# The key's rotation on all 128 partitions, in three steps, and the queries' rotation two gates earlier

## The chip, the cores and the metric

The kernel runs on one core of a Trainium2 chip. The metric is the device time of one execution in microseconds. The core has a matrix engine (TensorE, PE in the profile), three engines for elementwise work (VectorE or DVE, ScalarE or ACT, GpSimd or POOL), and a queue engine (SyncE, SP) that here only issues DMA transfers. Each engine works through its own list of instructions in a fixed order. PSUM holds what TensorE produces, in banks; a tile of 128x1024 takes two of them.

## What is computed

A two-layer encoder on one sequence of 1024 tokens with 1024 features. Each layer normalizes, projects into many pieces, runs two kinds of heads side by side, and projects back:

```
for i in range(DEPTH):                       # 2 layers
    u = rmsnorm(h, ln_mix[i]) @ w_in[i]
    c_q, c_kv, k_rope, gate_a, gq, gk, gv, lr_f, lr_b, gate_g = split_cols(u)
    y_mla = mla_branch(c_q, c_kv, k_rope, pos, ...) * silu(gate_a)
    y_gla = gla_branch(gq, gk, gv, lr_f, lr_b, ...) * silu(gate_g)
    h = h + concat(y_mla, y_gla) @ w_out[i]
    h = h + sigmoid(rmsnorm(h, ple_norm[i]) @ w_ple_gate[i]) * (p[i] @ w_ple_proj[i])

def apply_rope(x, pos):                      # 32 + 32 features, one angle per feature and token
    x1, x2 = x[..., :32], x[..., 32:]
    return concat([x1 * cos - x2 * sin, x1 * sin + x2 * cos])

# mla_branch: scores of 4 heads = q_nope . k_nope + q_rope . k_r, then softmax, then @ v
# q_rope = apply_rope(of each head's 64 features); k_r = apply_rope(k_rope), one for all heads
# gla_branch: linear attention with decay, forward and backward, in chunks of 64
```

The rotary key `k_rope` is one of the first things projected in a layer; its rotation is needed only by the scores.

## The kernel before

Activations lie with features on the partitions and tokens along the free dimension, so most tiles are 128x1024 f32. Each float operand of a product is split into a high and a low part (`wh`, `wl` for weights, `kh`, `kll` for keys, `qh`, `ql` for queries, `rh`, `rl` for the rotated queries, `ks`, `kl` for the rotated key), and a product is three matmuls: high by high, low by high, high by low. Splitting is a cast on ScalarE (L129, L132) and a subtraction on VectorE (L130, L133). Weights are loaded by SP into `wr` (L145) and split on ScalarE (L146, L150) and by GpSimd's accumulating DMA (L151); they rotate through two raw buffers and five split ones. Nearly all other tiles come from one ring of 41 buffers.

Within a layer the work is cut in steps. Two strings in `ORDER`, one for each layer, name them in the order in which they are handed to a scheduler, which then fixes each engine's list. A capital letter with a digit is a step: Q and K project queries and keys of the linear heads, V values, Z the decays of head i, S its states, O its output, G and A gate tiles, C and D latent tiles, N and M their norms. X (`q_pairs`) projects the rotary parts of all four heads into two PSUM tiles `xx` and loads the cosine and sine tables; E (`rotary_key`) rotates the key; T (`rotary_queries`) rotates the queries; H (`q_head`) and k (`make_k`) make one head's queries and keys; s, b, v and y are scores, turned probabilities, values and outputs of attention. A plus sign behind a step puts its PSUM tile into the other of two pools, `mm` and `aux`, of two tiles each. `xx` lives in `aux` until T has read it.

The steps around the change:

- `rotary_tables` (R) computes sine and cosine once, in a work tile whose 128 partitions hold 4 quarters of the tokens by 32 features (128x256), and writes them to device memory, `sind` and `cosd` (L278).
- X loads both tables back, four copies of 32x1024 each (L580).
- E works on rows 64 to 128 of `small`, the tile that holds the key's two halves of 32 features: four products, a difference and a sum on 32 partitions (L588 to L593), then two casts (L595, L596) and two subtractions (L598) that put the result twice into the 128 partitions of `ks` and `kl`.
- T reads `xx` (L613, L614, L615, twice), splits, and copies the parts to the tiles `qs` of four heads with sixteen copies on SP (L623).
- Scores `s0` (L672) of head 0 multiply, for each of 4 blocks of tokens and 2 halves of keys, `qh` and `ql` by `kh`, `qh` by `kll`, and `qs` by `ks` and by `kl`: 40 matmuls.
- Z (`gla_decay`): on ScalarE z, a, exp, log (L382 to L385), on VectorE z, two scans and more (L386 to L410). Its result goes through S and O to a norm that needs `sqh` (L132), `sql` (L133) and a product on TensorE (L185).

Of the kernel before, what the change touches and what calls it, by code (L numbers as in the profile page):

```python
# [46 lines left out]


WTAG = "aux"
ORDER = ("K0 R0 Q0 G0+ Z0 V0 K1 S0 Z1 V1 O0 S1 Q1 D0 Z2 G1 G2 P0 O1 S2 C0 Z3 D1 C1 N0 D2 O2 S3 G3 M0 A0 O3 X0 A1 E0 A2 A3+ H0 k0 T0 s0 v0 H2 k1+ s1 k2 b0 H1 k3 s2 y1 b1 H3+ s3 b2 v1 s4 y0 y3 b3 y2 s5 b4 w0 w1+ s6 w2 b5 w3+ s7 w4 b6 w5+ s8 w6 w7 b7",  # L50
         "Q0 K0 Z0 V0 S0 Z1 V1 S1 Q1 K1 Z2 G0 O0 S2 G1 Z3 G2+ C0 O1 D0 O2 S3 G3 C1 N0 D1 D2+ O3 M0 X0 A0 A1 E0 A2 k0 y2 H0 A3 T0 s0 v0 H3 k1+ s1 H1 b0 H2 s2 k2 b1 s3 y0 k3+ b2 v1 s4 y3 y1 b3 s5 b4 w0 w1+ s6 w2+ b5 w3 s7 w4 b6 w5+ s8 w6+ w7 b7")

ENG = dict(at="V", qi="V", qb="P", og="P", gate="P", sq="V", kT="A", put="A", o="A", ple="A", hadd="V")
TCKW = {"schedule_with_timeline_sim": True}
# [3 lines left out]
def hybrid_encoder(ctx: ExitStack, tc: tile.TileContext, xT, pT, pos, vecs, w_in, wq, wk, wv,  # L58
                   wz, w_out, w_gate, w_proj, outT, dbg=None):
    nc = tc.nc  # L60
    dbg = dbg or {}

    cp = ctx.enter_context(tc.tile_pool(name="const", bufs=1))
# [5 lines left out]
    def dram(shape, name):  # L69
        return tc.dram_tile(shape, F32, name=name)  # L70
# [49 lines left out]
    def mt(dt=F32, name="mt"):  # L120
        return rp.tile([P, S], dt, tag="r", name=name)
# [100 lines left out]
    h1d = dram([8, P, S], "h1d")  # L222
    cosd = dram([32, S], "cosd")
    sind = dram([32, S], "sind")

    def ple_projection(i):
        ops = []
# [12 lines left out]
        for g in range(4):  # L240
            hi, lo = load_split(w_proj[i, g], HC)
            for c in range(2):
# [4 lines left out]
                copy("ple", o, flat(ps))  # L247
                nc.sync.dma_start(projd[i][g * 2 + c], o)

    def rotary_tables():  # L250

        n = S // 4

        work = mt(name="rot")
        kk, ang, *rs = (work[:, i * n:(i + 1) * n] for i in range(4))
        posi = kk.bitcast(I32)
        for b in range(4):
            nc.sync.dma_start(posi[b * 32:(b + 1) * 32], pos[:, b * n:(b + 1) * n].to_broadcast((32, n)))
        nc.vector.tensor_copy(ang, posi)
        nc.vector.tensor_scalar(ang, ang, vec[:, V_INV:V_INV + 1], None, op0=ALU.mult)  # L260
        MAGIC = 12582912.0
        TWO_PI = 2.0 * np.pi
        C1 = 6.28125
        C2 = float(np.float32(np.round((TWO_PI - C1) * 2 ** 20) / 2 ** 20))
        C3 = float(np.float32(TWO_PI - C1 - C2))
        for r, dst, quarter in zip(rs, (sind, cosd), (0.0, 0.25)):
            nc.vector.tensor_scalar(kk, ang, 1.0 / TWO_PI, quarter, op0=ALU.mult, op1=ALU.add)
            nc.vector.tensor_scalar(kk, kk, MAGIC, None, op0=ALU.add)
            nc.vector.tensor_scalar(kk, kk, -MAGIC, None, op0=ALU.add)
            nc.vector.scalar_tensor_tensor(r, kk, -C1, ang, op0=ALU.mult, op1=ALU.add)  # L270
# [21 lines left out]
    for L in range(DEPTH):  # L292
# [231 lines left out]
        small, lr = in_small()  # L524
# [3 lines left out]
        def step(what, i):  # L528

            if what == "Q":  # L530
                qk["q", i] = in_qk(T_GQ, i, 64.0 ** -0.5)
            elif what == "K":
                qk["k", i] = in_qk(T_GK, i, 1.0, "mm" if i else "aux")
            elif what == "Z":
                dec[i] = gla_decay(i, qk["q", i // 2][i % 2], qk["k", i // 2][i % 2])
            elif what == "V":
                vals[2 * i], vals[2 * i + 1] = in_v(i)
            elif what == "S":
                sa[i] = gla_state(i, vals[i], dec[i])
            elif what == "O":  # L540
                gla_out(i, vals[i], dec[i][2], *sa[i], gg[i])
            elif what == "G":
                gg[i] = in_gate(T_GG, i, mt)
            elif what in "CD":
                raws[what].append(latent_tile((T_CKV if what == "C" else T_CQ) + i, sums[what]))
            elif what == "N":
                lat["C"] = latent_norm(raws["C"], sums["C"], V_KVN, 256)
            elif what == "M":
                lat["D"] = latent_norm(raws["D"], sums["D"], V_QN, 384)
            elif what == "A":  # L550
                in_ga(i)
# [20 lines left out]
        xx, ksl, qn, qs = [], [], {}, []  # L572
# [7 lines left out]
                    nc.sync.dma_start(t[b * 32:(b + 1) * 32], src)  # L580
            xx.extend(cs)

        def rotary_key():

            cos, sin = xx[2:]
            t1, t2 = mt(name="t1"), mt(name="t2")
            k1, k2 = slice(64, 96), slice(96, 128)
            nc.vector.tensor_tensor(t1[0:32], small[k1], cos[k1], op=ALU.mult)  # L588
            nc.vector.tensor_tensor(t2[0:32], small[k2], sin[k2], op=ALU.mult)
            nc.vector.tensor_tensor(t1[32:64], small[k1], sin[k1], op=ALU.mult)  # L590
            nc.vector.tensor_tensor(t2[32:64], small[k2], cos[k2], op=ALU.mult)
            nc.vector.tensor_tensor(t1[0:32], t1[0:32], t2[0:32], op=ALU.subtract)
            nc.vector.tensor_tensor(t1[32:64], t1[32:64], t2[32:64], op=ALU.add)  # L593
            ks, kl = mt(F32R, "ks"), mt(F32R, "kl")
            nc.scalar.activation(ks[0:64], t1[0:64], AF.Copy)  # L595
            nc.scalar.activation(ks[64:128], t1[0:64], AF.Copy)  # L596
            for half in (slice(0, 64), slice(64, 128)):
                nc.vector.tensor_tensor(kl[half], t1[0:64], ks[0:64].bitcast(F32), op=ALU.subtract)  # L598
            ksl.extend((ks, kl))

        def q_head(h):
            ps = q_tile(h, "mm")
# [345 lines left out]
```

## Time and profile before

| | us |
|---|---|
| median of 3 runs | 1459.65 |
| lowest and highest run | 1457.05, 1460.57 |
| the profiled execution | 1452.15 |
| its span | 1450.4 |
| TensorE busy | 1370.2 |
| VectorE busy | 857.9 |
| ScalarE busy | 720.8 |
| GpSimd busy | 428.2 |

The profile is of one execution. Its time is 1.75 us more than the span that the trace covers, and 7.5 us below the median of the other runs, so sums made from its rows are set against 1452.15. A row of the timeline gives start, duration, engine, line, operation and the tiles it writes and reads; in brackets stands how long the engine idled before it and what it then waited for. Consecutive rows of an engine can overlap a little, since instructions are pipelined. The granted clock is TensorE's, as a share of 2.4 GHz.

### The profile page before, as it was taken

Reading aid. Unit: us, or ns where it says so; the run is one execution under the profiler, and the core shown is the slowest. Engines: PE = TensorE matmul, PEld = TensorE weight load, DVE = VectorE, ACT = ScalarE, POOL = GpSimd, SP = SyncE. Lnnn points to the kernel's source line nnn. Section 1 sums busy time; section 2 is a strip of 40 time slices with the busy share of each in tenths; the row PEclk is TensorE's granted clock in tenths of the full one; section 3 lists DMA queues with packets and bytes.
Section 4 is the critical chain, followed back from the end, with each engine's and each line's share of the span. In section 5 each row is a group of like instructions: output and inputs, shape, how many; then the busy total and the mean of one; then the engine's idle time right before and its main releaser. Section 6 shows DMA issues by size and latency. Waiting matters only on the chain. (4 is left out here: it accounts for less than half of the span.)

```text
span 1450.4 us, 21078 instructions
## 1 busy us (share of the span) xinstructions
PE 1370.2 (94%) x8400; PEld 1162.2 (80%) x8400; DVE 857.9 (59%) x1196; ACT 720.8 (50%) x1013; POOL 428.2 (30%) x312
## 2 busy tenths in 40 slices
PE   8999899998899999999999999889989999999995
PEld 6799778877778788878889977678777888878995
DVE  2676745788446544374456667666744654446547
ACT  6565475544355443364445555634434553336542
POOL 4321211112346454012432202211234645301220
PEclk9999999999899999999999999999999999999998
DMA  8663445346432223345765343334752122325783
GB/s 294 176 129 76 111 109 168 82 101 143 132 71 56 61 78 84 77 102 147 208 170 114 80 99 73 74 89 90 180 133 63 43 74 66 95 66 110 190 190 119
DMA packets 77793, 163.93 MB, mean 113 GB/s; under 512 B 9536, under 2 KB 17088, under 8 KB 77696
## 3 DMA queue, kind: packets, MB, share of 16 engines
q1 hardware_dynamic: 51200, 116.19, 25.8%
q0 software_dynamic: 26496, 46.41, 19.0%
q8 instruction: 66, 1.08, 0.3%
q14 instruction: 31, 0.25, 0.1%
HBM read 128.74 MB, written 25.43 MB: 106 GB/s over the span
## 5 line engine op out<-in xcount | busy, mean ns | idle before, releaser
L150 ACT ACTIVATE wl<-wr 128x512 fp32r<-128x512 f32 (+2 forms) x176 | 107.4, 610 | 313.8 <-PE ps L171 280.4
L680 POOL TENSOR_SCALAR sc<-sc,sums 128x1024 f32<-128x1024 f32 x64 | 182.1, 2855 | 99.8 <-DVE sums L679 93.5
L151 POOL DMA_DIRECT2D wl<-in_w_in x84 | 72.7, 878 | 351.3 <-ACT wl L150 313.1
L146 ACT ACTIVATE wh<-wr 128x512 fp32r<-128x512 f32 (+2 forms) x184 | 110.8, 603 | 25.3 <-PE ps L171 11.9
L678 ACT ACTIVATE sc<-ps,top 128x1024 f32<-128x1024 f32 x64 | 71.4, 1115 | 71.3 <-DVE top L677 66.1
L677 DVE TENSOR_REDUCE top<-ps 128x1 f32<-128x1024 f32 x64 | 78.3, 1224 | 42.7 <-PE ps L672 42.5
L133 DVE TENSOR_TENSOR el<-ps,eh 128x1024 fp32r<-128x1024 f32 x64 | 78.1, 1220 | 40.4 <-ACT eh L132 40.2
L171 PE MATMUL ps<-x0h,wh 128*128 128x512 f32 x288 | 92.2, 402 | 9.8 <-DVE t L613 5.9
L171 PE MATMUL ps<-xh,wh 128*128 128x512 f32 x288 | 91.4, 397 | 9.8 <-DVE gate L366 4.6
L460 DVE SCALAR_TENSOR_TENSOR s<-s,last 64x128 f32<-64x128 f32 x208 | 77.0, 370 | 36.8 <-ACT s L102 29.9
L171 PE MATMUL ps<-x0h,wl 128*128 128x512 f32 x288 | 91.3, 398 | 0.0
L171 PE MATMUL ps<-xh,wl 128*128 128x512 f32 x288 | 90.9, 394 | 0.0
L171 PE MATMUL ps<-x0l,wh 128*128 128x512 f32 x288 | 90.6, 395 | 0.0
L171 PE MATMUL ps<-xl,wh 128*128 128x512 f32 x288 | 90.3, 393 | 0.0
L132 ACT ACTIVATE eh<-ps 128x1024 fp32r<-128x1024 f32 x64 | 65.4, 1022 | 38.9 <-PE ps L693 38.9
L171 PE MATMUL ps<-yh,wh 128*128 128x512 f32 x256 | 79.8, 393 | 1.2 <-DVE h L732 0.9
L151 POOL DMA_DIRECT2D wl<-in_w_out x32 | 27.9, 873 | 174.9 <-ACT wl L150 174.8
L171 PE MATMUL ps<-yh,wl 128*128 128x512 f32 x256 | 79.5, 390 | 0.0
L171 PE MATMUL ps<-yl,wh 128*128 128x512 f32 x256 | 79.5, 391 | 0.0
L171 PEld LDWEIGHTS ps<-x0h,wh 128*128 128x128 f32 x288 | 54.9, 193 | 22.1 <-DVE t L613 6.3
L693 PE MATMUL ps<-ident,sc 128*128 128x128 f32 x512 | 66.2, 273 | 6.2 <-DVE ql L130 3.1
L171 PEld LDWEIGHTS ps<-xh,wh 128*128 128x128 f32 x288 | 54.1, 191 | 22.3 <-DVE gate L366 5.0
(257 smaller groups left out, 3554.3 us busy)
## 6 DMA issues: line engine op xcount, KB each, us to landing
wr<-in_w_in SPq DMA_DIRECT2D x88, 256.0 KB, 3.3
wl<-in_w_in POOLq DMA_DIRECT2D x84, 256.0 KB, 4.8
wr<-in_w_gate SPq DMA_DIRECT2D x40, 256.0 KB, 3.2
projd<-po SPq DMA_DIRECT2D x16, 512.0 KB, 4.5
wr<-in_w_out SPq DMA_DIRECT2D x32, 256.0 KB, 3.3
wl<-in_w_out POOLq DMA_DIRECT2D x32, 256.0 KB, 4.7
wl<-in_w_gate POOLq DMA_DIRECT2D x32, 256.0 KB, 4.7
xraw<-in_xT SPq DMA_DIRECT2D x8, 512.0 KB, 5.4
```

Source lines behind the costliest of these rows:

```text
L132: nc.scalar.activation(hi, src, AF.Copy)
L133: nc.vector.tensor_tensor(lo, src, hi.bitcast(F32), op=ALU.subtract)
L146: nc.scalar.activation(hi[:, :n], raw[:, :n], AF.Copy)
L150: nc.scalar.activation(lo[:, :n], raw[:, :n], AF.Copy, scale=-1.0)
L151: nc.gpsimd.dma_start(lo[:, :n], src, accum_op=ALU.add)
L171: nc.tensor.matmul(ps[:, c, :], lhsT=a, rhs=b[:, c * HC:(c + 1) * HC], start=(i == 0 and j == 0), stop=(i == n - 1 and j == 2))
L460: nc.vector.scalar_tensor_tensor(state(n)[rows], state(m)[rows], alpha[rows, m:m + 1], state(n)[rows], op0=ALU.mult, op1=ALU.add)
L677: nc.vector.tensor_reduce(m, flat(ps), axis=AX.X, op=ALU.max, negate=True)
L678: nc.scalar.activation(e, flat(ps), AF.Exp, bias=m, accum_out=sums[:, b:b + 1])
L680: nc.gpsimd.tensor_scalar(e, e, sums[:, b:b + 1], None, op0=ALU.mult)
L693: nc.tensor.transpose(out=ps[:, j, b * P:(b + 1) * P], in_=e[:, kt], identity=ident)
```

## The change

The key's rotation becomes three steps in each layer. E0, early in the layer, copies the two halves of the key out of `small` into a tile `kr` in the tables' layout, 4 quarters by 32 features on 128 partitions. E1 rotates there, with the tables as the first computation left them (kept now in a tile `sc4`): six operations of 128x256, a split into `krp`, and eight copies to device memory `krd`. E2 loads `ks` and `kl` from there, each half of the partitions by a copy of its own. T0 stands in front of gates A2 and A3, E2 behind T0. In layer 0 A3 loses its plus sign and takes `mm` as the other gates do.

```
-ORDER = ("... G0+ Z0 V0 K1 S0 Z1 ... X0 A1 E0 A2 A3+ H0 k0 T0 s0 ...",
-         "... S0 Z1 V1 S1 Q1 ... A1 E0 A2 k0 y2 H0 A3 T0 s0 ...")
+ORDER = ("... G0+ E0 Z0 V0 K1 S0 E1 Z1 ... X0 A1 T0 E2 A2 A3 H0 k0 s0 ...",
+         "... S0 E0 Z1 V1 S1 E1 Q1 ... A1 T0 E2 A2 k0 y2 H0 A3 s0 ...")
+    krd = dram([DEPTH, 2, 2, 32, S], "krd")
+    sc4 = cp.tile([P, 2, S // 4], F32, name="sc4")
     def rotary_tables():
-        kk, ang, *rs = (work[:, i * n:(i + 1) * n] for i in range(4))
+        kk, ang = (work[:, i * n:(i + 1) * n] for i in range(2))
+        rs = sc4[:, 1], sc4[:, 0]
-        def rotary_key():
-            cos, sin = xx[2:]
-            t1, t2 = mt(name="t1"), mt(name="t2")
-            k1, k2 = slice(64, 96), slice(96, 128)
-            nc.vector.tensor_tensor(t1[0:32], small[k1], cos[k1], op=ALU.mult)
...
-            ks, kl = mt(F32R, "ks"), mt(F32R, "kl")
-            nc.scalar.activation(ks[0:64], t1[0:64], AF.Copy)
-            nc.scalar.activation(ks[64:128], t1[0:64], AF.Copy)
-            for half in (slice(0, 64), slice(64, 128)):
-                nc.vector.tensor_tensor(kl[half], t1[0:64], ks[0:64].bitcast(F32), op=ALU.subtract)
+        def rotary_key(part):
+            n = S // 4
+            if part == 0:
+                key["k"] = work = mt(name="kr")
+                for b in range(4):
+                    for i, row in enumerate((64, 96)):
+                        nc.sync.dma_start(work[b * 32:(b + 1) * 32, i * n:(i + 1) * n],
+                                          small[row:row + 32, b * n:(b + 1) * n])
+            elif part == 1:
+                k1, k2, u1, u2 = (key["k"][:, i * n:(i + 1) * n] for i in range(4))
+                rot = mt(name="krot")[:, :2 * n]
+                cos, sin = sc4[:, 0], sc4[:, 1]
+                for x1, x2, o, op in ((cos, sin, rot[:, :n], ALU.subtract), (sin, cos, rot[:, n:], ALU.add)):
+                    nc.vector.tensor_tensor(u1, k1, x1, op=ALU.mult)
+                    nc.vector.tensor_tensor(u2, k2, x2, op=ALU.mult)
+                    nc.vector.tensor_tensor(o, u1, u2, op=op)
+                parts = mt(F32R, "krp").rearrange("p (h c) -> p h c", h=2)
+                split(parts[:, 0], parts[:, 1], rot)
+                for i in range(2):
+                    for b in range(4):
+                        nc.sync.dma_start(krd[L, i, :, :, b * n:(b + 1) * n].rearrange("j f n -> f j n"),
+                                          parts[b * 32:(b + 1) * 32, i].bitcast(F32).rearrange("p (j n) -> p j n", j=2))
+            else:
+                for i, name in enumerate(("ks", "kl")):
+                    t = mt(F32R, name)
+                    for half in (slice(0, 64), slice(64, 128)):
+                        nc.sync.dma_start(t[half].bitcast(F32), krd[L, i].rearrange("j f n -> (j f) n"))
+                    ksl.append(t)
```

The lines of the kernel after are 5 to 20 higher than those of before: L382 is L387 there, L613 is L633, L623 is L643. Three places of the engines' lists show what the scheduler made of it. The first is ScalarE in layer 0 around the second decay step Z1. Before, behind the copies of head 0's states `s`:

```order
L102 ACTIVATE s_1022<-ps 64x128
L382 ACTIVATE z<-ps,vec 128x1024
L383 ACTIVATE a<-ps,vec 128x1024
L384 ACTIVATE a<-a 128x1024
L385 ACT_TABLE_LOAD
L385 ACTIVATE a<-a 128x1024
L150 ACTIVATE wl<-wr 128x512
L146 ACTIVATE wh<-wr 128x512
```

And after:

```order
L102 ACTIVATE s_1033<-ps 64x128
L132 ACTIVATE krp<-krot 128x512
L387 ACTIVATE z<-ps,vec 128x1024
L388 ACTIVATE a<-ps,vec 128x1024
L150 ACTIVATE wl<-wr 128x512
L146 ACTIVATE wh<-wr 128x512
L389 ACTIVATE a<-a 128x1024
L150 ACTIVATE wl<-wr 128x512
L146 ACTIVATE wh<-wr 128x512
L390 ACT_TABLE_LOAD
L390 ACTIVATE a<-a 128x1024
```

The cast `krp` of the rotated key now stands ahead of z, and two pairs of weight casts stand within the decay chain instead of behind it.

The second place is SP in layer 0, where the rotated queries go to their heads (`qs`, four tiles of four copies each; numbers tell buffers apart). Before, the last of them and what follows:

```order
L623 DMA qs_3427<-rh_3411 32x1024
L623 DMA qs_3427<-rl_3412 32x1024
L145 DMA wr_4006<-in_wq 128x384
L623 DMA qs_3427<-rh_3420 32x1024
L623 DMA qs_3427<-rl_3421 32x1024
L371 DMA gad0_339<-gate_3348 128x1024
```

And after:

```order
L145 DMA wr_4027<-in_wq 128x384
L643 DMA qs_3253<-rh_3247 32x1024
L643 DMA qs_3253<-rl_3248 32x1024
L643 DMA qs_3254<-rh_3238 32x1024
L643 DMA qs_3254<-rl_3239 32x1024
L643 DMA qs_3254<-rh_3247 32x1024
L643 DMA qs_3254<-rl_3248 32x1024
L618 DMA ks_3271<-krd_100 64x1024 x2
L618 DMA kl_3274<-krd_100 64x1024 x2
L376 DMA gad0_341<-gate_3407 128x1024
```

The loads of `ks` and `kl` stand behind all sixteen query copies, and the weight load `wr` stands ahead of six of those instead of two.

The third place is VectorE in layer 1, from the latent splits `cl` on. Before:

```order
L133 TENSOR_TENSOR cl<-craw,ch 128x1024 x2
L588 TENSOR_TENSOR t_8876<-small,cos 32x1024
L591 TENSOR_TENSOR t_8877<-small,cos 32x1024
L590 TENSOR_TENSOR t_8876<-small,sin 32x1024
L589 TENSOR_TENSOR t_8877<-small,sin 32x1024
L593 TENSOR_TENSOR t_8876<-t_8876,t_8877 32x1024
L592 TENSOR_TENSOR t_8876<-t_8876,t_8877 32x1024
L598 TENSOR_TENSOR kl<-t_8876,ks 64x1024 x2
L366 TENSOR_TENSOR gate<-ps,rstd 128x1024
L133 TENSOR_TENSOR kll<-ps,kh 128x1024
L133 TENSOR_TENSOR yl<-yraw,yh 128x1024
L130 SCALAR_TENSOR_TENSOR ql<-ps,qh 128x1024
```

And after:

```order
L133 TENSOR_TENSOR cl<-craw,ch 128x1024 x2
L633 TENSOR_TENSOR t_8924<-ps,cos 128x1024
L634 TENSOR_TENSOR t_8925<-ps,sin 128x1024
L635 TENSOR_TENSOR t_8924<-t_8924,t_8925 128x1024
L130 SCALAR_TENSOR_TENSOR rl<-t_8924,rh 128x1024
L633 TENSOR_TENSOR t_8933<-ps,sin 128x1024
L634 TENSOR_TENSOR t_8934<-ps,cos 128x1024
L371 TENSOR_TENSOR gate<-ps,rstd 128x1024
L635 TENSOR_TENSOR t_8933<-t_8933,t_8934 128x1024
L130 SCALAR_TENSOR_TENSOR rl<-t_8933,rh 128x1024
L133 TENSOR_TENSOR kll<-ps,kh 128x1024
L133 TENSOR_TENSOR yl<-yraw,yh 128x1024
```

The query rotation stands where the key rotation stood, and `kll`, the low part of head 0's keys, stands behind it.

## Rows read from the trace of the kernel before

**Rows 1.** The page: busy us (share of the span) and instructions of each engine.

```profile
PE 1370.2 (94%) x8400; PEld 1162.2 (80%) x8400; DVE 857.9 (59%) x1196; ACT 720.8 (50%) x1013; POOL 428.2 (30%) x312
```

**Rows 2.** Waits of TensorE, whole span: us in total, times, longest us.

```profile
PE ps L185 <- ACT sqh L132: 9.5, 5, 5.3
```

**Rows 3.** Timeline of TensorE, layer 0: start us, us, work, [idle before <- releaser].

```profile
357.53 0.50 PE L672 MATMUL ps<-kh,qh 128*128 128x512 f32 x1 [1.25 <-ACT kh L132]
...
366.72 1.22 PE L171 MATMUL ps<-x0h,wh 128*128 128x512 f32 x2 [5.85 <-DVE t L613]
...
387.21 0.39 PE L672 MATMUL ps<-ks,qs 128*128 128x512 f32 x1
...
387.66 0.62 PE L171 MATMUL ps<-ch,wh 128*128 128x512 f32 x2
```

**Rows 4.** Busy us (instructions) of PE, PEld, DVE, ACT, POOL; granted clock, DMA share, GB/s.

```profile
365.00:370.00 5.00, 3.28 (x8) 2.63 (x9) 4.03 (x4) 0.86 (x1) 0.00 (x0) 0.50 0.25 54
```

**Rows 5.** Timeline of VectorE, layer 0.

```profile
342.62 1.21 DVE L588 TENSOR_TENSOR t<-small,cos 32x1024 f32<-32x1024 f32 x1 [0.95 <-DMA cos<-cosd]
...
359.52 1.22 DVE L613 TENSOR_TENSOR t<-ps,cos 128x1024 f32<-128x1024 f32 x1
```

**Rows 6.** Timeline of TensorE, layer 1.

```profile
1033.13 0.61 PE L171 MATMUL ps<-cl,wh 128*128 128x512 f32 x2
...
1047.92 0.72 PE L171 MATMUL ps<-xh,wh 128*128 128x512 f32 x2 [1.49 <-DVE kll L133]
...
1067.28 0.77 PE L672 MATMUL ps<-ks,qs 128*128 128x512 f32 x1 [5.45 <-DMA qs<-rl]
...
1075.56 0.61 PE L171 MATMUL ps<-ch,wh 128*128 128x512 f32 x2
```

**Rows 7.** Timeline of VectorE, layer 1.

```profile
1050.46 1.21 DVE L613 TENSOR_TENSOR t<-ps,cos 128x1024 f32<-128x1024 f32 x1
```

**Rows 8.** Timeline of SP, layer 1: first and last of sixteen issues.

```profile
1061.87 0.56 SPq L623 DMA_DIRECT2D qs<-rh  x1
...
1071.92 0.60 SPq L623 DMA_DIRECT2D qs<-rl  x1
```

**Rows 9.** DMA issues, the page and 330 to 345 us: KB each, us to landing.

```profile
wr<-in_w_in SPq DMA_DIRECT2D x88, 256.0 KB, 3.3
...
sin<-sind SPq DMA_DIRECT2D x4, 128.0 KB, 5.4
```

**Rows 10.** Timeline of ScalarE and VectorE, layer 0, decay step Z1.

```profile
126.12 1.28 ACT L385 ACT_TABLE_LOAD   x1
127.41 1.06 ACT L385 ACTIVATE a<-a 128x1024 f32<-128x1024 f32 x1
130.63 0.63 ACT L150 ACTIVATE wl<-wr 128x512 fp32r<-128x512 f32 x1 [2.16 <-PE ps L352]
...
128.20 0.68 DVE L475 TENSOR_TENSOR at<-afb 128x512 f32<-128x512 f32 x1
...
130.84 1.23 DVE L386 SCALAR_TENSOR_TENSOR z<-z,a 128x1024 f32<-128x1024 f32 x1
```

**Rows 11.** Timeline of ScalarE and TensorE, layer 0, the norm behind.

```profile
147.00 1.06 ACT L132 ACTIVATE sqh<-o 128x1024 fp32r<-128x1024 f32 x1
...
151.68 0.39 PE L185 MATMUL ps<-sqh,ones_r 128*128 128x512 f32 x1
...
152.38 0.48 PE L185 MATMUL ps<-sql,ones_r 128*128 128x512 f32 x1
```

**Rows 12.** Timeline of ScalarE, TensorE and VectorE, layer 1, decay step Z2.

```profile
856.58 1.06 ACT L385 ACTIVATE a<-a 128x1024 f32<-128x1024 f32 x1
856.70 0.73 PE L171 MATMUL ps<-xh,wh 128*128 128x512 f32 x2 [1.80 <-DVE gqk L337]
...
859.19 1.23 DVE L386 SCALAR_TENSOR_TENSOR z<-z,a 128x1024 f32<-128x1024 f32 x1
...
877.86 0.50 PE L185 MATMUL ps<-sqh,ones_r 128*128 128x512 f32 x1 [0.46 <-ACT sqh L132]
```

More of the change, by code (lines that the diff above doesn't have):

```diff
@@ L49 @@
 WTAG = "aux"
-ORDER = ("K0 R0 Q0 G0+ Z0 V0 K1 S0 Z1 V1 O0 S1 Q1 D0 Z2 G1 G2 P0 O1 S2 C0 Z3 D1 C1 N0 D2 O2 S3 G3 M0 A0 O3 X0 A1 E0 A2 A3+ H0 k0 T0 s0 v0 H2 k1+ s1 k2 b0 H1 k3 s2 y1 b1 H3+ s3 b2 v1 s4 y0 y3 b3 y2 s5 b4 w0 w1+ s6 w2 b5 w3+ s7 w4 b6 w5+ s8 w6 w7 b7",
-         "Q0 K0 Z0 V0 S0 Z1 V1 S1 Q1 K1 Z2 G0 O0 S2 G1 Z3 G2+ C0 O1 D0 O2 S3 G3 C1 N0 D1 D2+ O3 M0 X0 A0 A1 E0 A2 k0 y2 H0 A3 T0 s0 v0 H3 k1+ s1 H1 b0 H2 s2 k2 b1 s3 y0 k3+ b2 v1 s4 y3 y1 b3 s5 b4 w0 w1+ s6 w2+ b5 w3 s7 w4 b6 w5+ s8 w6+ w7 b7")
+ORDER = ("K0 R0 Q0 G0+ E0 Z0 V0 K1 S0 E1 Z1 V1 O0 S1 Q1 D0 Z2 G1 G2 P0 O1 S2 C0 Z3 D1 C1 N0 D2 O2 S3 G3 M0 A0 O3 X0 A1 T0 E2 A2 A3 H0 k0 s0 v0 H2 k1+ s1 k2 b0 H1 k3 s2 y1 b1 H3+ s3 b2 v1 s4 y0 y3 b3 y2 s5 b4 w0 w1+ s6 w2 b5 w3+ s7 w4 b6 w5+ s8 w6 w7 b7",
+         "Q0 K0 Z0 V0 S0 E0 Z1 V1 S1 E1 Q1 K1 Z2 G0 O0 S2 G1 Z3 G2+ C0 O1 D0 O2 S3 G3 C1 N0 D1 D2+ O3 M0 X0 A0 A1 T0 E2 A2 k0 y2 H0 A3 s0 v0 H3 k1+ s1 H1 b0 H2 s2 k2 b1 s3 y0 k3+ b2 v1 s4 y3 y1 b3 s5 b4 w0 w1+ s6 w2+ b5 w3 s7 w4 b6 w5+ s8 w6+ w7 b7")
 ENG = dict(at="V", qi="V", qb="P", og="P", gate="P", sq="V", kT="A", put="A", o="A", ple="A", hadd="V")
@@ L558, in step @@
             elif what == "E":
-                rotary_key()
+                rotary_key(i)
             elif what == "H":
@@ L581, in q_pairs @@
             xx.extend(cs)
-        def rotary_key():
-            cos, sin = xx[2:]
-            t1, t2 = mt(name="t1"), mt(name="t2")
-            k1, k2 = slice(64, 96), slice(96, 128)
-            nc.vector.tensor_tensor(t1[0:32], small[k1], cos[k1], op=ALU.mult)
[L589 to L593, printed above, removed]
-            ks, kl = mt(F32R, "ks"), mt(F32R, "kl")
-            nc.scalar.activation(ks[0:64], t1[0:64], AF.Copy)
-            nc.scalar.activation(ks[64:128], t1[0:64], AF.Copy)
-            for half in (slice(0, 64), slice(64, 128)):
-                nc.vector.tensor_tensor(kl[half], t1[0:64], ks[0:64].bitcast(F32), op=ALU.subtract)
-            ksl.extend((ks, kl))
+        key = {}
```

## The prediction

> **What bounds the kernel now.** TensorE is the bound: it is busy for 1370.2 of the 1450.4 us [rows 1]. So a change can only win where TensorE waits or runs at half clock. I read its waits first, largest first. The largest, 9.5 us in five pieces, is for `sqh`, which ends each chain of the linear attention [rows 2]; it does not look like rotation at all, but the change puts new work in front of it. The next two are the rotation's own, one in each layer [rows 3, 6].
>
> Layer 0: the third gate tile A3 starts at 366.72 after 5.85 us of idling; it is held by a PSUM bank that the query rotation T0 has still to read. The first scores s0 end at 387.66 [rows 3]. From the idle on the granted clock is 0.50, the 1.2 GHz level [rows 4]. VectorE shows why T0 is late: the key's rotation begins at 342.62, T0 only at 359.52 [rows 5].
>
> Layer 1: A3 starts at 1047.92, s0 stalls for 5.45 us until 1067.28, waiting for the fourth piece of the rotated queries, and the next tile starts at 1075.56 [rows 6]. T0 begins at 1050.46 only [rows 7], and its sixteen copies leave SP one after the other from 1061.87 to 1071.92, so 10.05 / 15 = 0.67 us apart [rows 8].
>
> **Layer 1, rotation: gain 6.1.** The eight key instructions (some 1.22 us each) leave VectorE, and T0 stands directly behind the latent splits. X0's last products are at 1033.13 [rows 6], so its second tile can be read from about 1034, its first a little earlier. From there I walk with the durations of [rows 5], times of before throughout: two operations of 1.22, the cast on ScalarE (1.06, as that of [rows 10]) and the subtraction end the first half at about 1038.8; the second half, with gate A2 in the middle, ends at about 1046.3. The copies of the first head are issued by 1046.5. Then a weight load waits until H0 is done (about 1046.9: the 1.49 us of idle in front of A3 begin at 1046.4, and a cast lies between); the other twelve copies take 12 x 0.67 = 8.0 us, to about 1055, and the four new loads of `ks` and `kl` follow to about 1057. With 3.3 to 5.4 us to land [rows 9] they are there by 1060 to 1062.5.
>
> TensorE: `kll` moves behind T0's second half and is ready 1.4 us later, so A3 starts at 1049.3 instead of 1047.92 and ends at 1060.2. s0 first has nine products without rotation (2.0 us), to 1062.3. The 40 products at 0.227 us take 9.1 us: s0 ends at 1069.4 instead of 1075.56, a gain of **6.1**. If `kl` lands 1 us later it is 5, if `kll` is not late it is 7.5. The half clock behind the 5.45 us stall goes too and is contained in it.
>
> **Layer 0, rotation: gain 0.8.** Before, k0 ended at 356.28 (357.53 less its wait of 1.25), behind H0; a product takes 0.227 us (two of them 0.45) [rows 3], so H0 and k0, 18 and 12 products, are 6.8 us, and A2 ended at 349.4. Now A3 comes next, in a bank that nobody holds: 48 products, to 360.3; H0 to 364.4, k0 to 367.1. T0 reads X0 while A2 and A3 run and its second half is done at about 361. The 5.85 us wait is gone. But what is late next is the new load. On SP the order is fixed, and the weights in it wait for buffers: one for A3's end and the cast behind it (361), one for H0's (365), one for k0's (367.5). Six query copies stand behind the last, 6 x 0.67 = 4.0 us, then the two loads of `ks` and the two of `kl`; the last is issued at about 373.4. Landing is bounded by the 3.3 us of a weight tile of the same 256 KB and the 5.4 us of the `sin` table, which comes from device memory to part of the partitions as these do [rows 9]. I take 4.5, nearer the latter: 377.9. s0 has done its seven free products by then and idles some 7 us, so the half clock stays: 33 products, 7.5 us, plus 1.2 us (what layer 1 shows: 31 products from 1067.28 to 1075.56 are 8.28 us instead of 7.0). End 386.6 to 387.2, against 387.66: gain **0.8**; 2.2 if the loads land in 3.3, a loss of 0.5 if in 5.4 with a slow clock.
>
> The two loads of each tensor go to the two halves of the partitions. What the rows show of neighbouring copies is that they advance 0.67 us per 128 KB [rows 8]. The Trainium skill, DMA: Bandwidth & Descriptors, Rules for kernel authors, says that two transfers to disjoint halves of the partitions serialize, since both use the same engines, and that one transfer should be made. By it and the 0.67, the 1 MB would be there only at about 379, s0 would end at 388.3, and the sum below would be 1.5 us higher, still no change; no run here shows such loads.
>
> **Layer 0, the new step E1: costs 3.8.** Six products on 128 x 256, a cast, a subtraction. Their engine time is small: a product on 128 x 512 takes 0.68 [rows 10], so one on 128 x 256 lies between half of it, 0.34, and the whole; I take 0.36, since time here follows the elements of a partition. The place is what costs. On ScalarE the cast `krp` stands ahead of z and a of the second decay step, and waits for VectorE's last of the six. VectorE reaches them behind `at` (128.20, 0.68): four of the six and two state updates, 2.2 us, so `krp` starts at 131.1. Before, the chain's logarithm ended at 128.47, 2.4 us ahead of VectorE's use of it at 130.84 [rows 10]. Now: `krp` 0.63, z and a 2.1, a weight pair 1.1 (two casts like `krp`, overlapping), exp 1.06, a pair 1.1, the table 1.28, log 1.06 (durations of [rows 10]): 139.6, so VectorE's z moves from 130.84 to about 139.7, by 8.9.
>
> How much reaches TensorE? From VectorE's z to `sqh` there were 16.2 us, of which two weight pairs (2.1) now stand earlier: `sqh` goes from 147.00 to about 153.7 and its end to 154.8. TensorE used `sqh` from 151.68, so 3.6 us had been free; it now idles some 3.1, and the second operand `sql` (DVE, 1.23) lets it go on at about 156.2 instead of 152.38 [rows 11]. **3.8** lost; everything behind it is the same chain moved. Ends: 0 if `krp` isn't what starts z, 6 if the pairs don't help or a product costs the whole 0.68. SP issues the eight writes of `krd` in the same stretch, at some 0.6 us each; the weights queued behind come up to 5 us later, for a tile behind the one that runs (10.9 us for 48 products), and I count nothing. Without that cover it would be those 5.
>
> **Layer 1, E1: costs 2.8.** Here all four instructions (1.45 us) stand ahead of the four scalings of the keys for which TensorE waits (1.80 us, to 856.70). ScalarE's log ended at 857.64 and VectorE's z came at 859.19 [rows 12]. With `krp` at about 855.4, z, a, exp, the table and log end at 862.0: z moves by 2.8, `sqh` with it, and TensorE had no slack there (it waited 0.46 us for it). Ends: 1.45 (only the four instructions) and 4.
>
> **At no cost:** E0's eight copies of 32 KB, again some 5 us of SP in front of weights that are a tile ahead (5 without that cover); the casts of the old rotation, which leave ScalarE in a stretch where it waits; the sine tables, kept in a tile of their own.
>
> **Sum.** -6.1 - 0.8 + 3.8 + 2.8 = -0.3. The profiled execution took 1452.15 us (span 1450.4 and 1.75 around it); it would take 1451.9. The median of three runs is 1459.65, 7.5 higher, so the forecast is **1459.4**: no change. About 0.3% (4.4 us) is what a measurement of this kernel can tell from none.
>
> **Rivals.**
> (a) *The delay of E1 is absorbed*, since ScalarE or TensorE has other work there: then only -6.1 - 0.8 = -6.9, 1452.8. For it: VectorE and ScalarE are busy only half the time; against it: order within an engine is fixed, and z is next. With the loads in layer 0 early enough too (s0 from 370 to 379.5, gain 8) it is -14, 1445.6. That is the plain reading: both stalls vanish. Decided by whether `ks` and `kl` are issued before 366.
> (b) *E1's delay grows in layer 0*: if TensorE's gap before `sqh` comes to the size of the two that the clock halved behind, 5.85 in layer 0 and 5.45 in layer 1, it can halve here too. The price there was 1.2 us in layer 1, and at least 1.6 in layer 0 (3.28 us of products at half clock in one slice of 5 us [rows 4]). With 6 + 1.5 there, 4 in layer 1, a gain of 6.1 and none in layer 0: +5.4, 1465. Decided by that gap and the granted clock behind it.
> (c) *The new loads are late in both layers*, as layer 0's SP queue would have it: gain in layer 1 only 3, +2.8 in all, 1462.5; part of "no change".
>
> **Chances.** Forecast with (c) 0.40, (a) 0.33 (of it 0.08 with both stalls gone), (b) 0.27. Faster 0.33, same 0.40, slower 0.27. The range keeps (a) with a little more, and (b) to its upper end: 1449 to 1467; the forecast alone has 1455.5 to 1463.5.
>
> **What would show it.** Right: z of the second decay step on ScalarE directly behind `krp` at about 131.8; a new TensorE idle of 2 to 4 us before the `sqh` product near 152; no wait for `t` near 362, but one for `kl` of 5 to 8 us near 371 with the clock at half; in layer 1 no wait for `qs` and A3 starting near 1049 plus the shift. Wrong: z unmoved (then (a)); `ks` issued ahead of the copies of the last heads in layer 0; a wait for `ks` in layer 1.

## The result, and the profile after

The changed kernel takes 1468.18 us (median of 6 runs, 1465.0 to 1472.55), the kernel before 1457.7 in the same comparison (6 runs, 1455.84 to 1460.57): 1.0074 times as long, 95% interval 1.0059 to 1.0089. It is 10.5 us slower. The forecast of 1459.4 and its upper end of 1467 were both too low.

The profiled execution of after took 1465.0 us, its span is 1463.3, so 12.9 more than before. The page, first group, against [rows 1] (busy us, share, instructions):

```profile
PE 1377.2 (94%) x8400; PEld 1167.6 (80%) x8400; DVE 847.0 (58%) x1194; ACT 717.4 (49%) x1011; POOL 428.1 (29%) x312
```

VectorE has 11 us less to do, as meant. TensorE does the same 8400 products but is busy 7 us longer, at a mean granted clock of 0.981 instead of 0.985. Its waits over the whole span (us in total, times, longest), against [rows 2]:

```profile
PE ps L692 <- DMA ks<-krd: 9.4, 2, 8.2
PE ps L185 <- ACT sqh L132: 8.0, 5, 2.9
...
PE ps L692 <- DMA kl<-krd: 3.8, 2, 2.6
```

The waits for `t` and `qs` of [rows 3, 6] (5.85 and 5.45 us) are gone. The waits for the new loads, 13.2 us in four pieces, are new. Where they lie, on TensorE's timeline:

```profile
374.58 0.74 PE L692 MATMUL ps<-kh,qh 128*128 128x512 f32 x2 [2.50 <-ACT kh L132]
...
384.74 0.77 PE L692 MATMUL ps<-ks,qs 128*128 128x512 f32 x1 [8.19 <-DMA ks<-krd]
386.79 0.76 PE L692 MATMUL ps<-kl,qs 128*128 128x512 f32 x1 [1.28 <-DMA kl<-krd]
...
395.82 0.39 PE L171 MATMUL ps<-ch,wh 128*128 128x512 f32 x1
...
1060.82 0.72 PE L171 MATMUL ps<-xh,wh 128*128 128x512 f32 x2 [2.74 <-DVE kll L133]
...
1071.85 0.39 PE L692 MATMUL ps<-kh,qh 128*128 128x512 f32 x1
...
1072.30 0.39 PE L692 MATMUL ps<-kll,qh 128*128 128x512 f32 x1
1073.91 0.47 PE L692 MATMUL ps<-ks,qs 128*128 128x512 f32 x1 [1.22 <-DMA ks<-krd]
1076.94 0.77 PE L692 MATMUL ps<-kl,qs 128*128 128x512 f32 x1 [2.56 <-DMA kl<-krd]
...
1086.62 0.62 PE L171 MATMUL ps<-ch,wh 128*128 128x512 f32 x2
```

And the issues that these wait for, on SP's timeline. Of layer 0, the weight load ahead of the last six copies, the copy behind it, and the loads; of layer 1, against [rows 8], copies of the queries, the weight load among them, and the loads:

```profile
374.17 0.94 SPq L145 DMA_DIRECT2D wr<-in_wq  x1
375.15 1.23 SPq L643 DMA_DIRECT2D qs<-rh  x1
...
379.65 1.18 SPq L618 DMA_DIRECT2D ks<-krd  x2
380.93 1.18 SPq L618 DMA_DIRECT2D kl<-krd  x2
...
1055.92 0.55 SPq L643 DMA_DIRECT2D qs<-rh  x1
1056.52 1.12 SPq L643 DMA_DIRECT2D qs<-rl  x1
1057.69 1.24 SPq L643 DMA_DIRECT2D qs<-rh  x1
...
1059.68 0.52 SPq L145 DMA_DIRECT2D wr<-in_wq  x1
...
1068.02 0.59 SPq L643 DMA_DIRECT2D qs<-rl  x1
1068.66 1.24 SPq L618 DMA_DIRECT2D ks<-krd  x2
1069.93 1.23 SPq L618 DMA_DIRECT2D kl<-krd  x2
```

To lay both traces side by side I cut the span at TensorE waits that every kernel here has, and compare the stretches between them. "E1" stretches run from the wait for `afb` (127.57 and 811.76 in before) to the first gate wait of layer 0 (313.35) and to an `sqh` wait of layer 1 (928.11); "rotation" stretches from a gate wait (313.35, 969.24) to the wait for `ql` (405.23, 1093.01). Each kernel has one profile.

| stretch, us | before | after | difference | predicted |
|---|---|---|---|---|
| start, to `afb` of layer 0 | 127.57 | 130.68 | +3.1 | 0 |
| E1, layer 0 | 185.78 | 189.20 | +3.4 | +3.8 |
| rotation, layer 0 | 91.88 | 93.39 | +1.5 | -0.8 |
| between | 406.53 | 406.68 | +0.2 | 0 |
| E1, layer 1 | 116.35 | 119.34 | +3.0 | +2.8 |
| between | 41.13 | 41.27 | +0.1 | 0 |
| rotation, layer 1 | 123.77 | 123.50 | -0.3 | -6.1 |
| rest | 357.39 | 359.24 | +1.9 | 0 |

The first row is hardly the change's: a kernel that keeps the old key path (third run below) has 129.78 there, and the ten kernels of the experiments have 128.4 to 130.4. Nor, likely, is the last: from the wait for `ql` to the last wait for `acc`, near the end, they vary between 342 and 350 us, and I see no order in it that follows the edits. The change's own rows make 7.6 us.

### The profile page after: what moved, and what is told of

Same layout as the page of the kernel before. It is cut to its first block, busy times and chain, and to the rows that moved or that the text cites. A ratio compares the mean times of both kernels' runs of the same rounds, so it can differ in the third digit from the quotient of the medians.

```text
span 1463.3 us, 21147 instructions
## 1 busy us (share of the span) xinstructions
PE 1377.2 (94%) x8400; PEld 1167.6 (80%) x8400; DVE 847.0 (58%) x1194; ACT 717.4 (49%) x1011; POOL 428.1 (29%) x312
## 4 chain that ended last, share of the span: by engine, by line
PE 73%; DVE 11%; ACT 8%; DMA 5%; issue 2%; SPq 1%; POOL 0%; DVEq 0%; ACTq 0%
PE ps L171 43%; PE ps L692 10%; PE ps L731 6%; PE ps L357 5%; DVE s L465 4%; PE ps L713 3%; DMA wr<-in_w_gate 2%; PE ps L671 2%; PE ps L185 1%; ACT s L102 1%; PE ps L860 1%; SPq L643 1%; DMA kl<-krd 1%; DMA out<-fin 1%; PE ps L438 1%
## 5 line engine op out<-in xcount | busy, mean ns | idle before, releaser
L713 PEld LDWEIGHTS ps<-ident,sc 128*128 128x128 f32 x512 | 59.1, 140 | 14.8 <-DVE ql L130 3.6
```

Source lines behind the costliest of these rows:

```text
L713: nc.tensor.transpose(out=ps[:, j, b * P:(b + 1) * P], in_=e[:, kt], identity=ident)
```

## The experiments

The theory after the result: the gain is there but is held up by two things, (1) `ks` and `kl` are loaded too late, behind sixteen copies on SP, and (2) E1's cast stands ahead of the decay chain on ScalarE. The rival: the new path is dear in itself, or T0's move is what matters. Letters are those of the order: E2 are the loads, T0 the query rotation. Times are medians; the kernel before had medians of 1457.73, 1458.16 and 1456.47 beside them. The stretches of all runs stand in a table at the end of this section.

**The loads ahead of the query rotation.** In both layers of after:

```diff
-X0 A1 T0 E2 A2 A3
+X0 A1 E2 T0 A2 A3
```

> The changed kernel with one edit: the loads of ks and kl (E2) stand in front of the queries' rotation (T0), so that SP issues them before the sixteen query copies. Theory Q (the loads are late because of their place in SP's list): the waits for ks and kl (9.4 and 3.8 us in the changed kernel) vanish, s0 in layer 0 ends about 9 us earlier and in layer 1 about 5.8, so some 14 us less than the changed kernel's 1468.2: 1452 to 1456. Rival D (the copies and loads share one supply of DMA time, so that whatever is issued first makes the other late): the wait changes its name to qs and the time stays within 3 us of 1468. E1's cost stays in both: the sqh product of layer 0 is as late as in the changed kernel.

1456.1 us, ratio to before 0.9985 (0.997 to 1.0), so 12 us better than after. Layer 0 pays as meant: no wait for `ks` or `kl`, and the rotation takes 81.44 us, 10.4 less than before. Layer 1 gains nothing (124.13), where some 5.8 were expected. There the wait only moved. The new order's SP, ScalarE and TensorE in layer 1:

```profile
1029.76 1.26 SPq L618 DMA_DIRECT2D ks<-krd  x2
1031.13 1.22 SPq L618 DMA_DIRECT2D kl<-krd  x2
1033.55 0.36 SPq L145 DMA_DIRECT2D wr<-in_w_in  x1
...
1040.57 0.63 ACT L150 ACTIVATE wl<-wr 128x512 fp32r<-128x512 f32 x1 [4.74 <-DMA wr<-in_w_in]
...
1041.62 1.04 ACT L129 ACTIVATE rh<-t 128x1024 fp32r<-128x1024 f32 x1
...
1047.47 1.19 PE L171 MATMUL ps<-ch,wh 128*128 128x512 f32 x2 [3.70 <-DVE gate L371]
```

```profile
1048.00:1052.00 4.00, 4.00 (x11) 3.10 (x10) 1.68 (x2) 1.47 (x2) 0.00 (x0) 0.50 1.08 319
```

The last row is a window of 4 us (its start and end, length, busy us and instructions of five engines, granted clock, DMA share, GB/s). One MB stands ahead of the weight tile `wr`; that lands 7.0 us after its issue, where the page has 3.3 as its median. ScalarE waits for it with the cast of the rotated queries queued behind, VectorE's gate behind that, TensorE stalls 3.70, and behind the stall the clock is at 0.50.

**The key's cast on GpSimd.** After, with the first half of the split taken off ScalarE:

```diff
-split(parts[:, 0], parts[:, 1], rot)
+nc.gpsimd.tensor_copy(parts[:, 0], rot)
+nc.vector.tensor_tensor(parts[:, 1], rot, parts[:, 0].bitcast(F32), op=ALU.subtract)
```

> The changed kernel with one edit: the cast krp of the rotated key is made by GpSimd instead of ScalarE. Theory F (z and a of the next decay step wait behind krp in ScalarE's list): z runs about 8 us earlier in layer 0, the new idle of TensorE before the sqh and the gqk products there (1.42 and 1.50) goes, 3 to 4 us less in layer 0 and 1 to 2 in layer 1, in all 1462 to 1464. Rival V (what costs is VectorE's six new products and the subtraction, or SP's writes of krd): no less than 1467. If GpSimd's cast comes late, VectorE's subtraction waits for it in front of its z; then no gain either, and that wait is to be seen.

1458.4 us, ratio 1.0002 (0.9987 to 1.0018): about 10 us better than after, more than either expected. Of after and of this kernel, ScalarE around the second decay step of layer 0, and TensorE's wait behind it:

```profile
134.37 0.63 ACT L132 ACTIVATE krp<-krot 128x512 fp32r<-128x512 f32 x1 [9.83 <-DVE krot L607]
134.91 1.10 ACT L387 ACTIVATE z<-ps,vec 128x1024 f32<-128x1024 f32 x1
...
156.36 0.50 PE L185 MATMUL ps<-sqh,ones_r 128*128 128x512 f32 x1 [1.42 <-ACT sqh L132]
158.36 1.30 PE L425 MATMUL ps<-ident,gqk 128*128 128x128 f32 x5 [1.50 <-issue]
```

```profile
124.87 1.12 ACT L387 ACTIVATE z<-ps,vec 128x1024 f32<-128x1024 f32 x1 [1.46 <-PE ps L383]
...
137.12 1.22 DVE L391 SCALAR_TENSOR_TENSOR z<-z,a 128x1024 f32<-128x1024 f32 x1 [1.79 <-ACT a L390]
```

In after, ScalarE idled 9.83 us in front of the cast, with z queued behind it. Without the cast z runs 8.9 us earlier (10.0, of which 1.1 is the shift of the start), and TensorE has no wait for `sqh` there at all, although VectorE's z is still 4.3 us later than in before, counted from the wait for `afb`. E1 costs nothing in layer 0 (184.44 against 185.78 before); in layer 1 it costs 1.4, which the stretch behind gives back (39.70 against 41.13).

**Only T0 moved.** The kernel before, old key rotation kept, T0 directly behind it:

```diff
-X0 A1 E0 A2 A3+ H0 k0 T0 s0
+X0 A1 E0 T0 A2 A3 H0 k0 s0
...
-X0 A0 A1 E0 A2 k0 y2 H0 A3 T0 s0
+X0 A0 A1 E0 T0 A2 k0 y2 H0 A3 s0
```

> The kernel before with the second half of the change alone: the old key rotation on 64 partitions at its old place, directly behind it the queries' rotation, then gates A2 and A3 (A3 in the usual bank). Theory: moving T0 removes the waits for t in layer 0 and for qs in layer 1 (5.9 and 5.4 us and the half clock behind them) even with the old rotation in front, since its 12 us of VectorE end before A2 does in both layers: 8 us less in layer 0, 6 in layer 1, so 1444 against 1457.7. Then the whole loss is that of the new key path. Rival: the old rotation delays T0 so far that qs are late again; 1452 to 1458.

1459.31 us, ratio 1.0014 (1.0002 to 1.0026): no gain. TensorE in layer 1:

```profile
1060.31 1.22 PE L171 MATMUL ps<-xh,wh 128*128 128x512 f32 x2 [7.61 <-DVE kll L133]
```

The wait for `qs` became one for `kll`, since key rotation and query rotation now both stand ahead of it on VectorE. In layer 0 the wait for `t` is gone, but one of 2.78 us for `qs` stands in its place, and the stretch gains only 0.7. So the move alone doesn't pay while the key's rotation is on VectorE in front of it.

**The new key path, T0 at its old place.** The other half alone:

```diff
-X0 A1 T0 E2 A2 A3 H0 k0 s0
+X0 A1 E2 A2 A3+ H0 k0 T0 s0
...
-X0 A0 A1 T0 E2 A2 k0 y2 H0 A3 s0
+X0 A0 A1 E2 A2 k0 y2 H0 A3 T0 s0
```

> The other half of the change alone: the key's rotation in three steps (E2 where the old rotation stood), the queries' rotation behind k0 in layer 0 and behind A3 in layer 1 as before. Theory: E1's place costs 3.4 + 3.0 as in the changed kernel; the old stalls of T0 stay, since T0 is behind kll in VectorE's list, with 1 to 2 us gained in layer 0: 1457.7 + 6.4 - 1.5 = 1462.6. If the two halves simply added up (changed kernel +10.5, T0 moved alone +1.6), it would be +8.9: 1466.6.

1466.66 us, ratio 1.0058 (1.0036 to 1.008), where the additive rival put it. Its E1 stretches are longer by 4.9 and 3.0, and it has both old stalls again (4.96 for `t`, 5.36 for `qs`). The key path alone costs, and brings nothing until T0 moves.

**E1 late as well.** The first experiment with E1 moved from the decay step to in front of N0, in both layers:

```diff
-S0 E1 Z1
+S0 Z1
...
-C1 N0
+C1 E1 N0
```

> The changed kernel with two edits: E2 in front of T0 as in the first run, and E1 moved behind the last decay step and its state work, in front of the norm of the key's latents (N0), in both layers. Theories Q and F together: the waits for ks and kl gone (14 us) and E1's place no longer in front of a decay chain (3.4 in layer 0, 3.1 in layer 1): 1468.2 - 20 = 1448, from 1446 to 1451. If E1's cost is not its place but its work, 1453 to 1456.

1449.09 us, ratio 0.994 (0.9921 to 0.9959), as expected from place rather than work. In layer 0 E1 still lies within its stretch, which is only 0.8 longer than before; in layer 1 it has moved on into the rotation's stretch, and the one that it left is 0.5 longer than before. The rotation of layer 1, with E1 in it and the loads where the first experiment has them, takes 120.60, 3.5 less than there:

```profile
1040.47 0.70 PE L171 MATMUL ps<-ch,wh 128*128 128x512 f32 x2 [2.77 <-DVE gate L371]
```

```profile
1040.00:1044.00 4.00, 3.53 (x16) 2.93 (x17) 2.68 (x3) 2.12 (x2) 0.00 (x0) 1.00 1.10 271
```

The weight tile landed 6.0 us after its issue instead of 7.0, TensorE waited 2.77 for the gate instead of 3.70, and the clock stayed at 1.00. So what the first experiment lost against this one in layer 1 was wait and the clock behind it. Why the tile landed sooner isn't shown.

**The loads well ahead in layer 1.** The last kernel, with layer 1's loads 35 to 39 us earlier:

```diff
-D1 D2+ O3 M0 X0 A0 A1 E2 T0 A2
+D1 D2+ E2 O3 M0 X0 A0 A1 T0 A2
```

> The kernel of the run with E2 first and E1 late, with one more edit: in layer 1 E2 stands behind gate G... of the decay steps, ahead of the last output O3, some 50 us before the rotation. In the run with E2 first, layer 1 gained nothing although the waits for ks and kl were gone: the four loads, 1 MB, stood directly ahead of a weight load, which landed 7 us after its issue instead of 3; ScalarE's cast of that weight, the rotated query's cast behind it and gate A2 were late, and TensorE waited 3.7 us for that gate. Theory S (the loads only displace what is issued next, so a place with slack behind it costs nothing): the wait for gate A2 (2.8 us in the kernel before this edit) goes and layer 1's stretch from 969 us to the first turned probabilities, 120.6 us, gets 2.5 to 3 us shorter; 1445 to 1447 in all. Rival: gate A2 is late for another reason (VectorE's own order, T0 in front of the gate): 1448 to 1450 and the wait stays.

1444.6 us, ratio 0.9909 (0.9888 to 0.993). TensorE in layer 1 has the wait for `kll` that was predicted and none for gate, `qs`, `ks` or `kl`; the rotation takes 119.11. That is 1.5 less than in the kernel before it, where 2.5 to 3 were expected: behind the wait for `kll` the clock now fell, which it had not done there (1.00 from 1048 to 1052):

```profile
1042.93 0.73 PE L171 MATMUL ps<-xh,wh 128*128 128x512 f32 x2 [2.74 <-DVE kll L133]
```

```profile
1044.00:1048.00 4.00, 4.00 (x12) 3.17 (x11) 0.01 (x1) 0.00 (x0) 0.00 (x0) 0.57 0.90 225
```

**Both cures, the cast on GpSimd.** After, E1 at its place with its cast on GpSimd, layer 0's E2 ahead of T0, layer 1's behind N0:

```diff
-X0 A1 T0 E2 A2 A3
+X0 A1 E2 T0 A2 A3
...
-C1 N0 D1 D2+ O3 M0 X0 A0 A1 T0 E2 A2
+C1 N0 E2 D1 D2+ O3 M0 X0 A0 A1 T0 A2
```

> The changed kernel with three edits: the cast krp on GpSimd (E1 at its early place), E2 in front of T0 in layer 0, and E2 behind the latents' norm in layer 1, far ahead. If the costs found so far add up (about 10 for the cast's place, 14 for E2's), 1468.2 - 24 = 1444; 1442 to 1447. If E1's place and E2's place share a loss (the shifted chain gave room to the late loads), 1449 or more.

1441.27 us (1440.01 to 1442.88), ratio 0.9882 (0.9862 to 0.9903): 1.2% faster than before, and the best kernel here.

**One load of 128 partitions.** After, order unchanged; `krd` is written twice, and each of `ks` and `kl` is one transfer:

```diff
-for half in (slice(0, 64), slice(64, 128)):
-    nc.sync.dma_start(t[half].bitcast(F32), krd[L, i].rearrange("j f n -> (j f) n"))
+nc.sync.dma_start(t.bitcast(F32), krd[L, i].rearrange("c j f n -> (c j f) n"))
```

> The changed kernel, E2 at its place, but ks and kl each come by one transfer of 128 partitions (E1 writes its result to device memory twice) instead of two of 64. Same bytes loaded. If two transfers to halves of the partitions go one after the other, the waits for ks and kl (8.2 and 1.3 us in layer 0, 1.2 and 2.6 in layer 1) shrink by 1 to 2 us a layer: 1464 to 1467. If the bytes and the place in the queue set the landing, unchanged within 2 us: 1467 to 1469.

1458.31 us, ratio 1.0002 (0.9988 to 1.0017): 10 better than after, and better than both expected. In layer 1, SP and TensorE:

```profile
1065.09 0.58 SPq L616 DMA_DIRECT2D ks<-krd  x1
1065.71 0.45 SPq L616 DMA_DIRECT2D kl<-krd  x1
...
1070.79 0.50 PE L690 MATMUL ps<-kl,qs 128*128 128x512 f32 x1 [0.79 <-DMA kl<-krd]
```

The issue ends 4.6 us ahead of the product that waits for `kl`; in after it ended at 1071.16, 5.8 ahead. Two issues also take 1.1 us of SP, not 2.5. TensorE waits 0.79, not 3.78, keeps its clock (1.00 from 1070 to 1074), and the stretch takes 118.92, 4.6 less than after. Layer 0 gains 2.2; of its waits of 9.47 in after, 6.42 stay. The other 3 us of the 10 lie in the start and the rest.

**Two loads, all partitions.** The last kernel, but each tensor by two transfers of half the columns:

```diff
-    nc.sync.dma_start(t.bitcast(F32), krd[L, i].rearrange("c j f n -> (c j f) n"))
+    for half in (slice(0, HC), slice(HC, S)):
+        nc.sync.dma_start(t[:, half].bitcast(F32), krd[L, i].rearrange("c j f n -> (c j f) n")[:, half])
```

> As the run with one load of 128 partitions, but each of ks and kl comes by two transfers again, each of all 128 partitions by half of the tokens (256 KB as in the changed kernel). In the changed kernel the stretch in which ks and kl come in moved 225 to 240 GB/s with all DMA engines busy, in the run with one load 380 to 450 GB/s behind the copies. If the number of partitions a transfer reaches sets that rate, this kernel is as fast as the one with one load: 1458 to 1460, some 400 GB/s. If the number of transfers does (issues, or their fixed part), it is as slow as the changed kernel: 1466 to 1469, some 240 GB/s.

1463.36 us, ratio 1.0045 (1.0024 to 1.0066), between the two. Layer 1 takes as long as with the single load (119.40), though in another way: no wait for the loads, but the clock at 0.64 from 1062 to 1066, behind the wait for `kll`. Layer 0 is like after (93.80, waits of 5.46 and 2.21), and the rate there is 254, 191, 335 and 413 GB/s in the four windows of 2 us from 378 on, the later ones with the tiles behind the loads under way too, so it doesn't decide between the two expectations. How much of the gain is the count of transfers and how much the partitions stays open.

**One load on top of the best.** 

> The run with the cast on GpSimd and E2 ahead, plus one load of 128 partitions each. There is no wait for ks or kl left in it, so if DMA time is not what bounds the stretch around, nothing is to be gained: 1440 to 1443 as that run. If the loads still hold up weights there, 1437 to 1439.

The edits of both kernels together: 1442.87 us, ratio 0.9898 (0.9868 to 0.9929), not better than 1441.27. Loads that are early need no quick landing.

In the two kernels with E1 late, layer 1's E1 lies in the last column.

| kernel | E1, 0 | rotation, 0 | E1, 1 | rotation, 1 |
|---|---|---|---|---|
| before | 185.78 | 91.88 | 116.35 | 123.77 |
| after | 189.20 | 93.39 | 119.34 | 123.50 |
| loads ahead of T0 | 190.20 | 81.44 | 120.16 | 124.13 |
| cast on GpSimd | 184.44 | 92.97 | 117.77 | 123.23 |
| only T0 moved | 185.81 | 91.17 | 116.34 | 125.46 |
| key path alone | 190.69 | 92.38 | 119.36 | 124.36 |
| loads ahead, E1 late | 186.58 | 81.52 | 116.80 | 120.60 |
| and layer 1's loads well ahead | 186.50 | 81.44 | 116.81 | 119.11 |
| best: GpSimd, loads ahead | 185.32 | 82.91 | 117.76 | 119.24 |
| one load of 128 | 189.13 | 91.23 | 119.35 | 118.92 |
| two loads, all partitions | 189.06 | 93.80 | 119.32 | 119.40 |
| best with one load | 185.19 | 82.92 | 117.71 | 119.33 |

## Why the prediction was wrong, point by point

**Layer 1's rotation, -6.1 predicted, -0.3 measured: the step that failed.** The shift of layer 1 is 980.56 - 969.24 = 11.32 us. With it taken off, the first terms were right: A3 starts at 1049.5 (predicted 1049.3), the wait for `kll` is 2.74. The failed step is "the four new loads follow to about 1057" and "they are there by 1060 to 1062.5". T0's second half ends at 1046.4, as predicted, but the last load is issued by 1059.8, 2.8 later: three copies took 1.10 to 1.24 us instead of 0.67, the weight load among them 0.5 of SP that was not counted, and the four loads 2.5 instead of some 2. It lands 5.8 us after that, above the upper bound of 5.4, so `kl` is there at 1065.6. Nor were there nine products without rotation to bridge the wait, as in before: three stand ahead of the first with `ks`. s0 waits 1.22 and 2.56 us, and then runs at half clock, which the prediction had excluded with the wait (stretch, busy us and instructions of five engines, granted clock, DMA share, GB/s):

```profile
1076.00:1078.00 2.00, 1.06 (x3) 0.90 (x4) 0.00 (x0) 0.00 (x0) 0.00 (x0) 0.62 1.08 319
1078.00:1080.00 2.00, 2.00 (x6) 1.58 (x5) 0.12 (x1) 0.00 (x0) 0.00 (x0) 0.52 1.09 347
```

With `kl` there, 36 products of 0.227 us are left, 8.2 us; they take 9.68, to 1086.62. So 3.8 us of waiting and 1.5 of clock eat the gain; with nine products in front 31 would have been left behind `kl`, 1.1 us less. The mechanism held: in five kernels (the loads well ahead, the best, and the three with loads of all partitions) the stretch is 4.4 to 4.9 us shorter than before. Most of the 1.2 to 1.7 that are short of 6.1 is a term that the sum didn't have, the clock behind the wait for `kll`. With the loads well ahead A3 starts where it was predicted (1049.2 with that kernel's shift taken off), but takes 12.6 us instead of 10.9, at 0.57 for 4 us (the row of that run). In after and with one load the same wait of 2.74 and 2.73 left the clock at 1.00; with one load it is `kl` that is late.

**Layer 0's rotation, -0.8 predicted, +1.5 measured.** The picture was right: no wait for `t`, a long one for the new loads, the clock at 0.50 behind it. The size was off by the same term: shifted by 6.53 us, the weight load leaves at 367.6 (predicted 367.5) but takes SP 0.94, one copy 1.23, and the four loads 2.5, so the last issue ends at 375.6 (predicted 373.4), and `kl` is used from 380.3 (predicted 377.9).

**E1, +3.8 and +2.8 predicted, +3.4 and +3.0 measured: the size right, its make-up in layer 0 only half.** VectorE's z came at 139.3 without the shift of 3.1 (predicted 139.7), and TensorE idled 1.42 + 1.50 us before and behind the first products of the norm (predicted 3.1). But the clock fell there too:

```profile
156.00:160.00 4.00, 2.14 (x7) 1.61 (x8) 3.36 (x3) 1.35 (x3) 1.29 (x3) 0.79 0.35 79
160.00:164.00 4.00, 4.00 (x17) 3.22 (x16) 2.59 (x9) 1.02 (x1) 0.00 (x0) 0.78 0.28 52
```

That is 0.84 + 0.88 = 1.7 us of clock, where before shows 1.00. In return two later waits are shorter: 2.42 and 1.75 us for `s` and `gqk` in before, 1.97 and 0.89 in after. So the forecast's 3.8 was met partly by luck. In layer 1 VectorE's z came at 862.5 without the shift of 8.2 (predicted 862.0); the `sqh` product of [rows 12] came 4.0 later than before, and 1.0 of it was made up by the end of the stretch, where the wait for `sqh` is 2.89 us instead of 5.35. Four more kernels have the same E1 at the same place; their stretches are longer than before by 3.3 to 4.9 and 3.0 to 3.8, so tenths mean nothing here. The cast on GpSimd and the late E1 show that the place was the price.

**The sum.** The four terms make +7.6 and not -0.3; the two rotations miss by 8.1, the two E1 terms by 0.2 the other way. The medians differ by 10.5; the 3 us left over aren't told apart from the scatter of start and rest.

**The rivals.** (c), late loads in both layers, is what happened, but it was priced with 3 us of gain left in layer 1, of which 0.3 were left, and it was filed under "no change". It needed a chance of its own and the clock's price on top. (b) had a real mechanism at the wrong size: the clock fell behind two gaps of 1.42 and 1.50 us, not only behind one of 5.5, but cost 1.7 us, which the shorter later waits gave back; the sign came from the rotations. (a) was a real prospect, only not of this order: "both stalls vanish" gave 1445.6, and the kernels with the loads ahead and E1 out of the chain run at 1444.6 and 1441.27. "Decided by whether `ks` and `kl` are issued before 366" was the right question; the order printed ahead of the prediction already answered it.

**The rule on halves.** The prediction weighed what the Trainium skill states in DMA: Bandwidth & Descriptors, Rules for kernel authors, that two transfers to disjoint halves of the partitions should be one, and gave it 1.5 us (by its own landing, 1.1 later, it is 1.1). The run with one load agrees in direction; its size by the stretches is 2.2 us in layer 0 and 4.6 in layer 1.

## What to carry to other kernels

When work is moved out of a busy engine by way of device memory, the load at its end is the new deadline: place it by its position in the queue that issues it, not by the step it belongs to, and ask what it then stands in front of. An instruction that waits for another engine should not stand ahead of a chain on an in-order engine; an engine with nothing queued behind can do it: with the cast on GpSimd the chain's stretch was no longer than before in layer 0, and 1.4 us longer in layer 1. Halves of a change can each lose while both together, in the right order, win: here +1.6 and +8.5 us alone, +10.5 together as first ordered, -17 with both cures.

## What the runs showed of the hardware

With the DMA engines busy all the time, the rate still differs by transfer. Windows of after, layer 0, first while `ks` and `kl` land, then while the tiles issued behind them do:

```profile
382.00:384.00 2.00, 0.00 (x0) 0.00 (x0) 0.00 (x0) 0.00 (x0) 0.00 (x0) 0.50 1.04 238
384.00:386.00 2.00, 0.77 (x1) 0.29 (x1) 0.00 (x0) 0.00 (x0) 0.00 (x0) 0.50 1.03 240
386.00:388.00 2.00, 1.21 (x3) 1.05 (x4) 0.00 (x0) 0.00 (x0) 0.00 (x0) 0.50 1.01 406
```

At a DMA share of 1.0 the loads to 64 partitions move 240 GB/s; 2 us later, with the whole tiles `gad` and `yraw` under way, it is 406. Two of the kernels show it on the same bytes at the same place. In layer 1 of the best kernel, and of the best with one load, `ks` and `kl` come in with little else under way:

```profile
987.00:990.00 3.00, 3.00 (x125) 2.86 (x128) 2.57 (x3) 2.78 (x4) 0.86 (x1) 1.00 1.04 232
```

```profile
987.00:989.00 2.00, 2.00 (x58) 1.66 (x58) 1.71 (x2) 2.00 (x3) 0.86 (x1) 1.00 1.02 407
```

In the first, each tensor comes by two loads to 64 partitions, and they move 232 GB/s; in the second it comes by one load to all 128, and these move 407. The DMA share shows no difference (1.04 and 1.02), so here it doesn't tell what the loads move. In after `kl` landed 5.8 us behind the last issue, where [rows 9] had 3.3 and 5.4 us.

The clock behind a wait was not the same each time: behind 2.74 us for `kll` it was 0.57 for 4 us with the loads well ahead, and 1.00 in after.
